# Moving the low weight parts by 64 bytes, spreading out a series, and splitting a last block in an fp32r encoder kernel

## The chip, the cores and the metric

The kernel runs on one core of a Trainium2 chip, as one program and one launch. The metric is the time on the device in microseconds (us), from start to end of one execution. The core has a matrix engine (PE, with its weight loads shown as PEld), a vector engine (DVE), an activation engine (ACT), GpSimd (POOL) and a queue engine (SP) that here only issues DMAs. Matmul results go to PSUM, which the kernel uses as eight banks of 512 fp32 columns on 128 partitions; all else lies in SBUF.

## The reference

The input is one sequence of 256 tokens of width 2048. Two layers follow each other, each with a residual addition, and a last norm ends it:

```python
h = rmsnorm(x, norm_w[0]);  x = x + mamba2_mixer(h, ...)
h = rmsnorm(x, norm_w[1]);  x = x + forgetting_attention_mixer(h, ...)
return rmsnorm(x, final_norm_w)        # x * rsqrt(mean(x*x) + 1e-6) * w
```

The Mamba-2 mixer projects to z, x, B, C (width 10240) and 64 step sizes dt, runs a causal convolution of four taps with SiLU, takes `dt = softplus(dt_raw + bias)`, runs the chunked state-space sum over 8 groups of 8 heads, gates with SiLU(z), applies a norm in each group, and projects 4096 back to 2048. The forgetting attention projects to q, k, v, z (4 x 4096) and 32 forget logits, takes `log_sigmoid` of these and their running sum, runs causal softmax attention with that sum as bias, gates with SiLU(z), and projects back. Everything is fp32.

## The kernel before, in words

**fp32 by parts.** Nearly all the weight products are made in the fp32r type, with each weight tile split into a high part `wh` (ACT, `act_hi`, L100) and a low part `wl` (DVE, `dve_lo`, L106: raw minus high). The activations are split the same way. A product is then the sum of high*high, low*high and high*low.

**The stream of weights.** Weights come in halves of 128 x 1024 fp32 (512 KB). `prep` (L130) takes a `raw` buffer (seven of them), issues the load on SP, and lets ACT and DVE make `wh` (five buffers) and `wl` (four buffers, `bufs=4` at L135 and L156). All three lie in the pool "weights". `raw`, `wh` and `wl` are each 4096 bytes a partition, so all of them start at the same place within 4096 bytes.

**The order of work.** The whole program is a list of parts (`run`, L162). A part is one half of a weight unit. For each part `run` first emits the preparation of the half that lies three ahead, then the part's matmuls, then its `post`, and then whatever was put off until now with `later(n, fn)` (L121), n counted in parts. The order that is emitted is a priority: a scheduler then sets the fixed order of each engine's queue from it, by when it reckons things to be ready. On the chip each queue runs in that order.

**Three kinds of parts.** `unit_t` (L190) makes a transposed output tile: the weight tile is the stationary operand, eight matmuls with `wh` on 512 columns (both activation parts side by side, L203) and eight with `wl` on 256 columns (L207). `units_a` (L267) has the activations stationary and the weights moving: twelve matmuls of 512 columns for a half, the `wl` ones last (L282), into one PSUM bank for each of the two token tiles. `sum_units` (L691) makes most of the two output projections (groups 0 to 5) by a Strassen-like scheme, from weight tiles that accumulating DMAs on POOL's queue add up in SBUF, six matmuls a part: for each p the three products high*wh, low*wh, high*wl (L711).

**Step sizes and forget gates.** `per_token` (L326) turns the 64 (or 32) columns to tokens and hands them to `decays` (L422) or `forget` (L800). Both call `log1p_exp` (L309): on DVE ten small dependent instructions after an Exp on ACT, L314 to L323, ending in the series of L320 to L323. Then come `dts` (L425) and `dta` (L430), and five parts later `decay_sums` (L435): small matmuls on `dta` (L440 on), a copy, and a write of the running sums to DRAM (`acs_d`).

**The sums by head.** `load_acs` (L519) reads the running sums of two heads back, broadcast to 128 partitions, into one of two `acsB` buffers, on POOL's DMA queue. `decay` (L561) makes exponentials from it on ACT (L566, L568), DVE multiplies (L572), and `y_pe` (L577) uses the product on PE (L585).

**The end.** The last output block (group 7, columns 1536 to 2047, `n == 3`) is made for the first token tile and then for the second (`by_token`). `finish` (L976) is called for each block and token tile after the sum into `xs` (L677). For the first three blocks it squares on ACT and multiplies by the norm weight on DVE. For the last it squares (L756), sums the four squares (L984), takes the power -0.5 (L114 on DVE, L115 on POOL), scales four quarters (two on DVE at L987 and L988, two on ACT at L990) and issues four output DMAs on SP (L992).

Of the kernel before, what the change touches and what calls it, by code (L numbers as in the profile page):

```python
# [63 lines left out]
def hybrid_kernel(ctx: ExitStack, tc: tile.TileContext, a):  # L64
# [7 lines left out]
    wp = pool("weights", 5)  # L72
    cp = pool("const", 1)
# [14 lines left out]
    nhalf = cp.tile([P, 2], F32, name="nhalf")  # L88
# [41 lines left out]
    def prep(u, h, pieces=1):  # L130


        raw = wp.tile([P, 1024], F32, tag="raw", name="raw", bufs=RAW)
        wh = wp.tile([P, 1024], F32R, tag="wh", name="wh")
        wl = wp.tile([P, 1024], F32R, tag="wl", name="wl", bufs=4)  # L135
        for i in range(pieces):
            c = slice(i * 1024 // pieces, (i + 1) * 1024 // pieces)
            nc.sync.dma_start(raw[:, c], u["src"][:, h * 1024 + c.start:h * 1024 + c.stop])
            act_hi(wh[:, c], raw[:, c])
            dve_lo(wl[:, c], raw[:, c], wh[:, c])  # L140
            if i + 1 < pieces:
                yield
        u["w"][h] = (wh, wl)

    def prep_sum(u):
# [10 lines left out]
        wl = wp.tile([P, 1024], F32R, tag="wl", name="wl", bufs=4)  # L156
# [110 lines left out]
    def units_a(srcs, act, post, by_token=False):  # L267


        held = {}  # L270
# [3 lines left out]
        def mm(n, tiles):  # L274
            if n == 0 and tiles[0] == 0:
                held["ps"] = [bank(psm, f"psa{t}") for t in range(T2)]
            wh, wl = us[n // 2]["w"][n % 2]
            for i, w in enumerate((wh, wh, wl)):
                for k2 in range(2):
                    c = slice(k2 * 512, k2 * 512 + 512)  # L280
                    for t in tiles:
                        nc.tensor.matmul(held["ps"][t], act(2 * n + k2, t)[i % 2], w[:, c],  # L282
                                         start=n == k2 == i == 0,
                                         stop=n == n_h - 1 and k2 == 1 and i == 2)

        parts = []
        for tiles in ((0,), (1,)) if by_token else ((0, 1),):
            for n in range(n_h):
                parts.append({"u": us[n // 2], "h": [n % 2],
                              "mm": lambda n=n, tiles=tiles: mm(n, tiles)})  # L290
            parts[-1]["post"] = lambda tiles=tiles: post(held["ps"], tiles)
# [17 lines left out]
    def log1p_exp(v, n, name):  # L309
# [10 lines left out]
        nc.vector.tensor_scalar(q, s2, 2.0 / 17, None, op0=ALU.mult)  # L320
        for d in (15, 13, 11, 9, 7, 5, 3):
            nc.vector.scalar_tensor_tensor(q, q, 2.0 / d, s2, op0=ALU.add, op1=ALU.mult)
        nc.vector.scalar_tensor_tensor(q, q, 2.0, s, op0=ALU.add, op1=ALU.mult)  # L323
        return q
# [40 lines left out]
    rst1 = cp.tile([P, 2], F32, name="rst1")  # L365
# [56 lines left out]
    def decays(v):  # L422
        v = v.rearrange("p t h -> p (t h)")
        l = log1p_exp(v, T2 * MH, "sp")
        nc.vector.scalar_tensor_tensor(dts.rearrange("p t h -> p (t h)"), v, 0.0, l,  # L425
                                       op0=ALU.max, op1=ALU.add)
# [3 lines left out]
        nc.vector.scalar_tensor_tensor(  # L430
            dta, dts, -1.0, na.unsqueeze(1).to_broadcast([P, T2, MH]),
            op0=ALU.mult, op1=ALU.mult)
        later(5, lambda: decay_sums(dta))
# [47 lines left out]
    def group_units(g):  # L481
# [37 lines left out]
        def load_acs(i):  # L519
            acs = lp.tile([P, 2, S], F32, tag="acsB", name="acsB", bufs=2)  # L520
# [149 lines left out]
    def out_units(w, act, groups, done, enter=None):  # L670

        parts = []
        for n in range(4):
            def post(pss, tiles, n=n):
                for t in tiles:
                    c = xs[:, t, n * 512:(n + 1) * 512]
                    nc.vector.tensor_tensor(c, pss[t], c, op=ALU.add)  # L677
                    if done is not None:
                        done(n, t)
# [11 lines left out]
    def sum_units(w, held, groups):  # L691
# [3 lines left out]
        for cp2 in range(2):  # L695
# [7 lines left out]
            def mm(u, form, name, start, stop, ps=ps):  # L703
# [96 lines left out]
    def forget(v):  # L800
        vf = small.tile([P, T2 * FH], F32, tag="vf", name="vf", bufs=1)
        nc.vector.tensor_copy(vf.rearrange("p (t h) -> p t h", t=T2), v)
        l = log1p_exp(vf, T2 * FH, "ls")
        lf = small.tile([P, T2, FH], F32, tag="lf", name="lf", bufs=1)
        nc.vector.scalar_tensor_tensor(lf.rearrange("p t h -> p (t h)"), vf, 0.0, l,
                                       op0=ALU.min, op1=ALU.subtract)
        later(5, lambda: forget_sums(lf))
# [168 lines left out]
    def finish(n, t):  # L976
        square(n, t)
        c = xs[:, t, n * 512:(n + 1) * 512]
        fw = lay2["fw"]
        if n < 3:  # L980
            nc.vector.tensor_tensor(c, c, fw, op=ALU.mult)
            return
        r = small.tile([P, 1], F32, tag="fr", name="fr")
        nc.vector.tensor_reduce(r, lay2["sq"][:, t, :], axis=mybir.AxisListType.X, op=ALU.add)  # L984
        rsqrt(r, r, 1.0 / D, EPS)
        quarter = [xs[:, t, m * 512:(m + 1) * 512] for m in range(4)]
        nc.vector.tensor_scalar(quarter[2], quarter[2], r, None, op0=ALU.mult)  # L987
        nc.vector.scalar_tensor_tensor(c, c, r, fw, op0=ALU.mult, op1=ALU.mult)  # L988
        for m in range(2):
            nc.scalar.activation(quarter[m], quarter[m], AF.Copy, scale=r)  # L990
        for m in (2, 0, 3, 1):
            nc.sync.dma_start(a["out"][t * P:(t + 1) * P, m * 512:(m + 1) * 512], quarter[m])  # L992
# [100 lines left out]
```

## Time and profile before

| | |
|---|---|
| median of 3 runs | 1622.39 us (1622.38 to 1625.78) |
| the profiled execution | 1623.64 us, of which its span is 1621.8 us |
| busy, share of the span | PE 99%, PEld 85%, DVE 78%, ACT 62%, POOL 8% |
| granted TensorE clock | 0.998 |
| DMA | 347.70 MB, 214 GB/s on average |
| matmuls and weight loads | 8514 each |

The span is what the profile covers; the rest of an execution's time lies around it. A row of the timeline gives the start, the time to the end of the last of its merged instructions, the engine, the line and operation, the tile written and those read, the shapes, the count, and in brackets how long the engine had been idle and what ended that. Matmuls are pipelined: one that takes 0.39 us from start to end starts 0.23 us after the one before it. The pace of the engine is therefore read from starts, and not from durations.

### The profile page before, as it was taken

To read this page: it belongs to the slowest core of one execution; us is meant where nothing else is said; L and a number is where in the kernel's file an instruction comes from. 1 tells how busy PE (TensorE), PEld (TensorE's weight loads), DVE (VectorE), ACT (ScalarE), POOL (GpSimd) and SP (SyncE) were. 2 spreads that over 40 slices of the span, in tenths; PEclk is the share of its full clock that TensorE was granted. 3 is DMA by queue.
4 is the path that set the end of the run, shared out by engine and by line. 5 is a ranking of instruction groups with operands and counts; after the bars stand their busy time and mean duration, and the time that the engine had idled before them with its cause. 6 is when DMAs were issued, how large, how long until landed. Compare 5 with 4: busy or idle time off the path is not lost.

```text
span 1621.8 us, 23800 instructions
## 1 busy us (share of the span) xinstructions
PE 1598.9 (99%) x8514; PEld 1371.1 (85%) x8514; DVE 1263.8 (78%) x2091; ACT 1002.7 (62%) x1609; POOL 122.1 (8%) x166
## 2 busy tenths in 40 slices
PE   8999999999999999999999999999999999999997
PEld 6788888888888888888888888888888888888886
DVE  6898989898989897757767677676787676786776
ACT  7677777676767665645555566565565565665653
POOL 0000111011101110000000010100000000101000
PEclk9999999999999999999999999999999999999999
DMA  9666789778977897555555687865887866878752
GB/s 354 203 204 195 200 251 227 256 192 250 234 250 192 246 229 229 173 183 196 179 189 179 204 227 228 223 225 177 223 233 214 238 205 188 223 220 238 222 180 98
DMA packets 96937, 347.70 MB, mean 214 GB/s; under 512 B 11153, under 2 KB 11793, under 8 KB 96817
## 3 DMA queue, kind: packets, MB, share of 16 engines
q1 hardware_dynamic: 78768, 282.09, 51.3%
q0 software_dynamic: 18048, 64.07, 21.6%
q8 instruction: 67, 1.10, 0.3%
q14 instruction: 54, 0.43, 0.1%
HBM read 343.92 MB, written 2.20 MB: 213 GB/s over the span
## 4 chain that ended last, share of the span: by engine, by line
PE 88%; issue 4%; DMA 3%; DVE 2%; ACT 1%; POOL 0%; SPq 0%; ACTq 0%; POOLq 0%; DVEq 0%
PE pst L203 30%; PE psa L282 23%; PE pst L207 16%; PE psx L711 7%; PE psz L711 4%; PE psv L711 2%; PE py L585 2%; DVE wl L106 1%; DMA raw<-in_wf_q 1%; PE ppt L922 1%; DMA cst<-in_consts 1%; DMA xs<-in_x 1%; PE pyt L640 0%; PE pof L590 0%; PE pxa L538 0%
## 5 line engine op out<-in xcount | busy, mean ns | idle before, releaser
L106 DVE TENSOR_TENSOR wl<-raw,wh 128x1024 fp32r<-128x1024 f32 (+1 forms) x453 | 552.1, 1219 | 212.2 <-PE pst L207 85.8
L100 ACT ACTIVATE wh<-raw 128x1024 fp32r<-128x1024 f32 (+1 forms) x453 | 478.1, 1057 | 352.3 <-PE pst L203 133.3
L203 PE MATMUL pst<-x,wh 128*128 128x512 f32 x2272 | 575.3, 394 | 3.0 <-ACT v L102 3.0
L203 PEld LDWEIGHTS pst<-x,wh 128*128 128x128 f32 x2272 | 412.0, 188 | 80.1 <-ACT v L102 3.6
L207 PEld LDWEIGHTS pst<-x,wl 128*128 128x128 f32 x2272 | 309.8, 190 | 22.4
L207 PE MATMUL pst<-x,wl 128*128 128x256 f32 x2272 | 316.6, 282 | 0.0
L282 PE MATMUL psa<-wh,x 128*128 128x512 f32 x1024 | 260.2, 395 | 0.0
L282 PEld LDWEIGHTS psa<-wh,x 128*128 128x128 f32 x1024 | 189.7, 188 | 40.6 <-issue 1.9
L106 DVE TENSOR_TENSOR wl<-sum_a,wh 128x1024 fp32r<-128x1024 f32 x96 | 117.2, 1221 | 36.9 <-PE pst L207 23.7
L100 ACT ACTIVATE wh<-sum_a 128x1024 fp32r<-128x1024 f32 x96 | 101.6, 1058 | 64.0 <-PE psa L282 27.1
L282 PE MATMUL psa<-wl,x 128*128 128x512 f32 x512 | 137.1, 390 | 1.2 <-DVE wl L106 1.2
L282 PEld LDWEIGHTS psa<-wl,x 128*128 128x128 f32 x512 | 96.0, 188 | 21.6 <-DVE wl L106 1.7
L106 DVE TENSOR_TENSOR wl<-sum_b,wh 128x1024 fp32r<-128x1024 f32 x48 | 58.6, 1222 | 21.9 <-PE pst L207 11.6
L100 ACT ACTIVATE wh<-sum_b 128x1024 fp32r<-128x1024 f32 x48 | 50.9, 1061 | 31.7 <-PE psa L282 9.6
L153 POOL DMA_DIRECT2D sum_a<-in_wf_s x36 | 31.2, 866 | 338.7 <-DVE wl L106 238.5
L263 ACT COPY rest<-pst 128x256 f32<-128x256 f32 (+2 forms) x146 | 52.2, 358 | 3.1 <-PE pst L252 1.5
L566 ACT ACTIVATE ee<-acsB,beta 128x128 f32<-128x128 f32 x128 | 42.6, 391 | 10.6 <-DMA acsB<-acs_d 6.2
L153 POOL DMA_DIRECT2D sum_a<-in_wm_s x36 | 31.4, 873 | 203.1 <-DVE xT L468 70.3
L468 DVE SCALAR_TENSOR_TENSOR xT<-cu,vec,xT 128x255 f32<-128x255 f32 (+2 forms) x96 | 45.5, 474 | 0.4 <-ACT xT L463 0.4
L908 ACT ACTIVATE uu<-uu,mx 128x128 f32<-128x128 f32 x64 | 28.5, 446 | 25.7 <-DVE mx L906 25.7
L711 PE MATMUL psx<-wh,ghf 128*128 128x512 f32 x96 | 38.3, 399 | 0.0
L711 PE MATMUL psx<-wh,glf 128*128 128x512 f32 x96 | 37.8, 393 | 0.0
(312 smaller groups left out, 2025.8 us busy)
## 6 DMA issues: line engine op xcount, KB each, us to landing
raw<-in_wm_t SPq DMA_DIRECT2D x90, 512.0 KB, 5.0
raw<-in_wm_z SPq DMA_DIRECT2D x64, 512.0 KB, 5.3
raw<-in_wf_q SPq DMA_DIRECT2D x64, 512.0 KB, 4.5
raw<-in_wf_k SPq DMA_DIRECT2D x64, 512.0 KB, 4.6
raw<-in_wf_v SPq DMA_DIRECT2D x64, 512.0 KB, 4.1
raw<-in_wf_z SPq DMA_DIRECT2D x64, 512.0 KB, 4.4
sum_a<-in_wm_s POOLq DMA_DIRECT2D x36, 512.0 KB, 5.9
sum_a<-in_wf_s POOLq DMA_DIRECT2D x36, 512.0 KB, 5.6
```

Of the source, the lines that this page charges most:

```text
L100: nc.scalar.activation(out, in_, AF.Copy)
L106: nc.vector.tensor_tensor(out, in_, hi.bitcast(F32), op=ALU.subtract)
L153: nc.gpsimd.dma_start(u["sums"][name], src, accum_op=ALU.add)
L203: nc.tensor.matmul(ps, wh[:, k8 * P:k8 * P + P], v[:, k].rearrange("p i s -> p (i s)"), start=k == 0, stop=False)
L207: nc.tensor.matmul(ps[:, S:], wl[:, k8 * P:k8 * P + P], v[:, k, 0], start=False, stop=k == KT - 1)
L263: nc.scalar.copy(rest, ps[:n, S:])
L282: nc.tensor.matmul(held["ps"][t], act(2 * n + k2, t)[i % 2], w[:, c], start=n == k2 == i == 0, stop=n == n_h - 1 and k2 == 1 and i == 2)
L468: nc.vector.scalar_tensor_tensor(acc[:, j:], u[:, :S - j], cw(3 - j), acc[:, j:], op0=ALU.mult, op1=ALU.add)
L566: nc.scalar.activation(ee[:, j, t, :], st["acs"][i][:, j, t * P:t * P + P], AF.Relu, scale=-1.0, bias=beta[:, t, h:h + 1])
L585: nc.tensor.matmul(st["py"][t][:, c], m[:, j, t, :], st["xd"][:, t, c], start=True, stop=True)
L711: nc.tensor.matmul(ps[name], y[:, form, :], w[:, c], start=start and p == i == 0, stop=stop and p == 1 and i == 2, skip_group_check=True)
L908: nc.scalar.activation(uu[:, c:c + n], uu[:, c:c + n], AF.Exp, bias=mx[:, t:t + 1], accum_out=sm[:, t:t + 1])
```

## The change

**Low parts.** `wl` moves from the pool "weights" to a pool of its own, "lows", with four buffers as before. A pool "between" lies ahead of it and holds two small tiles, `nhalf` and `rst1`, that the pool "const" held: 32 bytes a partition each, so every `wl` starts 64 bytes further on than it did, and `raw` and `wh` stay where they were. What lies behind "const" starts where it did, but for the pools behind "small", which grows by two 32-byte buffers.

**Series.** `log1p_exp` stops after the square s2; the series, and what uses it, is emitted one part later, and `decay_sums` and `forget_sums` four parts after that.

**First group's running sums.** For group 0 `load_acs` takes its tile from the `gh` buffers of the pool "forms", which hold nothing yet, in place of the two `acsB` buffers.

**Order in `sum_units`.** The six matmuls of a part go by product and then by p, so that both `wl` products come last.

**The end.** The last block goes in three pieces: first token tile (512 columns), second token tile columns 0 to 255, then 256 to 511, the two halves in the same PSUM bank. The sum of the first three squares is formed after the third block. The last square (or its two halves) is added to it. Of the first tile only quarter 0 is scaled at once; quarter 3 is emitted after the addition of the last half, quarters 2 and 1 after the second tile's power.

```diff
+    mp = pool("between", 1)
+    lo = pool("lows", 4)
     cp = pool("const", 1)
...
-    nhalf = cp.tile([P, 2], F32, name="nhalf")
+    nhalf = mp.tile([P, 2], F32, name="nhalf")
...
-        wl = wp.tile([P, 1024], F32R, tag="wl", name="wl", bufs=4)
+        wl = lo.tile([P, 1024], F32R, tag="wl", name="wl")
...
         def mm(n, tiles, a, b):
+            if n == a == 0:
+                for t in tiles:
+                    held[t] = bank(psm, f"psa{t}")
...
-                        nc.tensor.matmul(held["ps"][t], act(2 * n + k2, t)[i % 2], w[:, c],
+                        nc.tensor.matmul(held[t][:, a:b], act(2 * n + k2, t)[i % 2], w[:, c],
...
-        for tiles in ((0,), (1,)) if by_token else ((0, 1),):
+        for tiles, a, b in ((((0,), 0, 512), ((1,), 0, 256), ((1,), 256, 512)) if by_token else
+                            (((0, 1), 0, 512),)):
...
-        nc.vector.tensor_scalar(q, s2, 2.0 / 17, None, op0=ALU.mult)
...
+        def series():
+            nc.vector.tensor_scalar(q, s2, 2.0 / 17, None, op0=ALU.mult)
+            for d in (15, 13, 11, 9, 7, 5, 3):
+                nc.vector.scalar_tensor_tensor(q, q, 2.0 / d, s2, op0=ALU.add, op1=ALU.mult)
+            nc.vector.scalar_tensor_tensor(q, q, 2.0, s, op0=ALU.add, op1=ALU.mult)
+            done(q)
+        later(1, series)
...
-        later(5, lambda: decay_sums(dta))
+            later(4, lambda: decay_sums(dta))
...
-            acs = lp.tile([P, 2, S], F32, tag="acsB", name="acsB", bufs=2)
+            if g == 0:
+                acs = gp.tile([P, 896], F32, tag="gh", name="acsB0")
+                acs = acs[:, :2 * S].rearrange("p (h s) -> p h s", h=2)
+            else:
+                acs = lp.tile([P, 2, S], F32, tag="acsB", name="acsB", bufs=2)
...
-                for p in range(2):
-                    gh, gl = held[u["g"]][p]
-                    c = slice(p * 512, p * 512 + 512)
-                    for i, (y, w) in enumerate(((gh, wh), (gl, wh), (gh, wl))):
+                for i, w in enumerate((wh, wh, wl)):
+                    for p in range(2):
+                        y = held[u["g"]][p][i % 2]
+                        c = slice(p * 512, p * 512 + 512)
...
+            if n == 2:
+                lay2[f"sum{t}"] = r = small.tile([P, 1], F32, tag="fr", name="fr")
+                nc.vector.tensor_reduce(r, lay2["sq"][:, t, :3], axis=mybir.AxisListType.X,
+                                        op=ALU.add)
+                nc.vector.tensor_scalar(r, r, D * EPS, None, op0=ALU.add)
...
+        if b0 == 512 and t == 1:
+            lay2["scale"](3)
+        q = small.tile([P, 1], F32, tag="fq", name="fq")
+        junk = sp.tile([P, 512], F32, tag="zth", name="junkf")
+        nc.scalar.activation(junk[:, :b0 - a0], xs[:, t, 1536 + a0:1536 + b0], AF.Square,
+                             accum_out=q)
+        if b0 < 512:
+            nc.vector.tensor_tensor(r, r, q, op=ALU.add)
+            return
+        nc.vector.tensor_scalar(q, q, r, 1.0 / D, op0=ALU.add, op1=ALU.mult)
+        nc.gpsimd.tensor_tensor(r, q, nhalf[:, :1], op=ALU.pow)
+        if t == 0:
+            lay2["scale"] = scale
+            scale(0)
+        else:
+            for m in (2, 1):
+                lay2["scale"](m)
+            for m in (2, 0, 3, 1):
+                scale(m)
```

`scale(m)` scales quarter m on ACT (0 and 1) or DVE (2 and 3) and issues its output DMA.

More of the change, by code (lines that the diff above doesn't have):

```diff
@@ L272, in units_a, with mm @@
         us = [{"src": src, "w": [None, None]} for src in srcs]
-        def mm(n, tiles):
-            if n == 0 and tiles[0] == 0:
-                held["ps"] = [bank(psm, f"psa{t}") for t in range(T2)]
+        def mm(n, tiles, a, b):
+            if n == a == 0:
+                for t in tiles:
+                    held[t] = bank(psm, f"psa{t}")
             wh, wl = us[n // 2]["w"][n % 2]
@@ L673, in out_units, with post @@
         for n in range(4):
-            def post(pss, tiles, n=n):
+            def post(pss, tiles, a=0, b=512, n=n):
                 for t in tiles:
-                    c = xs[:, t, n * 512:(n + 1) * 512]
-                    nc.vector.tensor_tensor(c, pss[t], c, op=ALU.add)
-                    if done is not None:
+                    c = xs[:, t, n * 512 + a:n * 512 + b]
+                    nc.vector.tensor_tensor(c, pss[t][:, a:b], c, op=ALU.add)
+                    if enter is not None:
+                        done(n, t, a, b)
+                    elif done is not None:
                         done(n, t)
@@ L974, in load_fw, with finish, scale @@
         nc.gpsimd.dma_start(fw, a["fnw"][n * 512:(n + 1) * 512].partition_broadcast(P))
-    def finish(n, t):
-        square(n, t)
-        c = xs[:, t, n * 512:(n + 1) * 512]
+    def finish(n, t, a0, b0):
         fw = lay2["fw"]
+        part = lambda m: xs[:, t, m * 512:(m + 1) * 512]
         if n < 3:
-            nc.vector.tensor_tensor(c, c, fw, op=ALU.mult)
-            return
[L983 to L992, printed above, removed]
+            square(n, t)
+            nc.vector.tensor_tensor(part(n), part(n), fw, op=ALU.mult)
+            if n == 2:
[3 more added lines that the diff above has]
+                nc.vector.tensor_scalar(r, r, D * EPS, None, op0=ALU.add)
+            return
+        r = lay2[f"sum{t}"]
+        def scale(m):
+            if m < 2:
+                nc.scalar.activation(part(m), part(m), AF.Copy, scale=r)
+            elif m == 2:
+                nc.vector.tensor_scalar(part(2), part(2), r, None, op0=ALU.mult)
+            else:
+                nc.vector.scalar_tensor_tensor(part(3), part(3), r, fw, op0=ALU.mult,
+                                               op1=ALU.mult)
+            nc.sync.dma_start(a["out"][t * P:(t + 1) * P, m * 512:(m + 1) * 512], part(m))
+        if b0 == 512 and t == 1:
[12 more added lines that the diff above has]
+            scale(0)
+        else:
+            for m in (2, 1):
+                lay2["scale"](m)
+            for m in (2, 0, 3, 1):
+                scale(m)
```

39 lines of the change are left out of this document (19 added, 20 removed).

## The prediction

> **What bounds the kernel now.** I read the page first (busy shares and the chain that ended last), then what PE waited for, then the timeline around each of its waits, and last the end.
>
> ```profile
> span 1621.8 us, 23800 instructions
> PE 1598.9 (99%) x8514; PEld 1371.1 (85%) x8514; DVE 1263.8 (78%) x2091; ACT 1002.7 (62%) x1609; POOL 122.1 (8%) x166
> ...
> PE 88%; issue 4%; DMA 3%; DVE 2%; ACT 1%; POOL 0%; SPq 0%; ACTq 0%; POOLq 0%; DVEq 0%
> ...
> L207 PE MATMUL pst<-x,wl 128*128 128x256 f32 x2272 | 316.6, 282 | 0.0
> ```
>
> PE is busy for 1598.9 of 1621.8 us, and the chain is PE's. So time can come from two places only: the 23 us in which PE stands (10 of them behind its last matmul, below), or the pace at which it runs. Two of the waits that the profile lists for PE (total, times, longest):
>
> ```profile
> PE py L585 <- DVE ee L572: 1.5, 1, 1.5
> PE psa L282 <- DVE wl L106: 1.2, 1, 1.2
> ```
>
> Each is a single wait, both in the first group, as the timeline shows further down. Now the pace, from starts:
>
> ```profile
> 1302.96 1.98 PE L203 MATMUL pst<-x,wh 128*128 128x512 f32 x8
> 1304.78 1.11 PE L207 MATMUL pst<-x,wl 128*128 128x256 f32 x8
> 1305.73 2.00 PE L203 MATMUL pst<-x,wh 128*128 128x512 f32 x8
> ```
>
> Eight matmuls of 512 columns take 1.82 us (228 ns each), eight of 256 columns 0.95 us (119 ns). Half of 228 is 114, so a short matmul with `wl` as its stationary operand costs 5 ns more than its columns alone would, 2272 times: 11.4 us. Something that goes with each weight load is in that, and the shift touches these loads.
>
> **The change part by part.** *Low parts 64 bytes on.* No instruction is added or taken away; the address of 2272 stationary tiles changes (L207), and that of the moving operand where `wl` is that. Does an address that is no multiple of 128 bytes cost PE anything? The nearest rows are attention's small products: adding up the tiles of the pools puts that pool 32 bytes past a multiple of 128, and both operands of L884 and L885 lie in it.
>
> ```profile
> 751.97 0.28 PE L884 MATMUL psc<-kh,qh 128*128 128x256 f32 x1
> 752.08 0.28 PE L885 MATMUL psc<-kl,qh 128*128 128x256 f32 x1
> 752.20 1.98 PE L203 MATMUL pst<-x,wh 128*128 128x512 f32 x8
> ```
>
> They run 0.11 and 0.12 us apart, 115 ns on average: no dearer than the 119 ns of L207, and a little under it. But there both operands have the same offset, and behind the change `wl` and `x` differ by 64 bytes, which no row shows. So the bounds are 5 ns less for each of the 2272 (-11.4 us, the long matmul's pace) and as much more (+11.4 us, nothing shows more). I take 0, as the rows with an odd start are nearest and differ by a few ns in a count of two. DVE's writing of `wl` and the loads of `raw` keep their work; they run beside PE.
>
> *The series one part later.* In the first layer `wl` came late to the first half of z:
>
> ```profile
> 51.35 0.28 DVE L322 SCALAR_TENSOR_TENSOR sp_q<-sp_q,sp_s 128x128 f32<-128x128 f32 x1
> 51.55 0.48 DVE L468 SCALAR_TENSOR_TENSOR xT<-cu,vec,xT 128x254 f32<-128x254 f32 x1
> 51.95 0.28 DVE L323 SCALAR_TENSOR_TENSOR sp_q<-sp_q,sp_s 128x128 f32<-128x128 f32 x1
> 52.15 0.48 DVE L468 SCALAR_TENSOR_TENSOR xT<-cu,vec,xT 128x253 f32<-128x253 f32 x1
> 52.54 0.28 DVE L425 SCALAR_TENSOR_TENSOR dts<-v,sp_q 128x128 f32<-128x128 f32 x1
> 52.74 1.22 DVE L106 TENSOR_TENSOR wl<-raw,wh 128x1024 fp32r<-128x1024 f32 x1
> 53.88 0.28 DVE L430 SCALAR_TENSOR_TENSOR dta<-dts,na 128x128 f32<-128x128 f32 x1
> 54.08 0.42 DVE L264 TENSOR_TENSOR cu<-pst,rest 128x256 f32<-128x256 f32 x1
> ```
>
> ```profile
> 55.14 0.65 PE L440 MATMUL pc<-cst,dta 128*64 128x128 f32 x4
> ```
>
> DVE runs these back to back, and each step of the series holds it 0.20 us (51.35 to 51.55). Were the three that stand here (51.35, 51.95, 52.54) behind the L106 at 52.74 in place of ahead of it, `wl` would come 0.6 us earlier, and of PE's 1.2 us wait 0.6 would be left. But something else is late next: `dta` was done at 54.16 and PE used it at 55.14, 1 us later. With PE 0.6 us ahead and three to five steps of 0.2 us now behind, that slack is used up, and L440 could wait for some 0.6 us; what is queued behind it on PE is the next half of z. So between -1.2 (wait gone, L440 in time) and +0.3 us (L440 waits longer than L282 did). I take -0.6, as the slack of 1 us covers about the rest. In the second layer the same step has no wait among PE's, so it brings 0 there.
>
> *Group 0's own buffers.* POOL issued the third load when ACT let go of the first buffer, and ACT then stood:
>
> ```profile
> 68.29 0.40 ACT L566 ACTIVATE ee<-acsB,beta 128x128 f32<-128x128 f32 x1 [1.11 <-DMA acsB<-acs_d]
> ...
> 73.09 0.40 ACT L566 ACTIVATE ee<-acsB,beta 128x128 f32<-128x128 f32 x1 [1.75 <-DMA acsB<-acs_d]
> ```
>
> ```profile
> 71.08 0.43 DVE L473 SCALAR_TENSOR_TENSOR xT<-cu,xT 128x256 f32<-128x256 f32 x1 [4.63 <-ACT cu L470]
> ...
> 77.42 0.68 DVE L572 TENSOR_TENSOR ee<-ee,cb 128x512 f32<-128x512 f32 x1
> ```
>
> ```profile
> 78.24 0.96 PE L585 MATMUL py<-xd,ee 128*128 128x64 f32 x7 [1.46 <-DVE ee L572]
> ```
>
> The 1.75 us go, since loads three and four no longer wait. The 1.11 us are for the second load, which had its buffer, and stay. PE's 1.46 us follow from DVE, which worked without a stop from 71.08, when a tanh released it, to the L572 that PE wants. That stretch begins before the wait that goes. So the gain reaches PE only if the scheduler, seeing the exponentials ready earlier, puts L572 further ahead: between 0 and -1.46 us, and I take -0.5, nearer to 0 by the timeline. Behind PE's wait stands the next unit's L203. The `gh` buffers are wanted long after.
>
> *Order in `sum_units`.* The low part is needed after four matmuls and not after two, 0.46 us later. No wait for it stands among PE's at L711, so 0.
>
> *The end.* Before:
>
> ```profile
> 1611.26 0.61 PE L282 MATMUL psa<-wl,ghf 128*128 128x512 f32 x2
> ...
> 1612.27 0.75 DVE L988 SCALAR_TENSOR_TENSOR xs<-xs,fr,fw 128x512 f32<-128x512 f32 x1
> ...
> 1612.93 0.68 DVE L677 TENSOR_TENSOR xs<-psa,xs 128x512 f32<-128x512 f32 x1
> 1613.71 0.63 ACT L756 ACTIVATE junkb<-xs 128x512 f32<-128x512 f32 x1 [0.51 <-DVE xs L677]
> ...
> 1614.65 0.15 DVE L114 TENSOR_SCALAR fr<-fr 128x1 f32<-128x1 f32 x1
> 1614.89 0.55 POOL L115 TENSOR_TENSOR fr<-fr,nhalf 128x1 f32<-128x1 f32 x1 [3.06 <-DVE fr L114]
> 1615.48 1.34 ACT L990 ACTIVATE xs<-xs,fr 128x512 f32<-128x512 f32 x2 [1.05 <-POOL fr L115]
> ```
>
> From the last matmul's end (1611.87) to the scaling (1615.48) are 3.61 us, of which DVE spent 1.06 on the first tile's quarters before it could add. After: an addition of 256 columns (0.42, as L264 above) with a hand-off of 0.1 on each side (1613.61 to 1613.71), a square of 256 columns with the reading of its sum (between half of 0.63 and all of it; 0.52 as an estimate), one DVE step of 0.15, POOL with its hand-offs 0.68 (1614.80 to 1615.48): 1.97 us, so 1.64 less. Against it: 24 matmuls of 119 ns in place of 12 of 228 ns are 0.12 us. And the second half goes into the bank that DVE is reading the first half from. No row of before shows an engine reading a bank while PE writes it, so the price lies between 0 and a full wait: last matmul 0.28, addition 0.42 and two hand-offs (0.10 and 0.14, the latter from L572's end at 78.10 to 78.24), less one normal step of 0.12, or 0.8 us. I take the 0.8, since the two halves are one tile to whatever orders the accesses: -1.64 + 0.12 + 0.8 = -0.7. The four outputs of the second tile are issued as before. Ends: -1.5 without that wait, and 0 where the first tile's quarter 3 (0.75, L988) still stands ahead of the last addition.
>
> That reading and writing one bank at once is no choice of order alone is said by the Trainium skill ("PSUM — Partial Sum Buffer", PSUM bank collisions raise a hardware error): two engines on one bank and quarter of the partitions collide, whatever columns they touch, so software has to keep them apart. By that rule the halves run one behind the other and the end gives 0.7; without it, 1.5. No run here shows it yet.
>
> The sum: 0 - 0.6 - 0.5 + 0 - 0.7 = -1.8 us. The profiled execution took 1623.64 us (span 1621.8 and 1.84 around it), so 1621.8 for it; it lies 1.25 us above the median of 1622.39, which gives 1620.6. About 0.2% (3.2 us, below 1619.15 or above 1625.6) is what a measurement of this kernel can tell from no change, so this is no change by that measure.
>
> **The rivals.** *The loads of `wl` run faster.* If the 5 ns of each short matmul come from the weight load and the moving operand reading the same place in step, 64 bytes part them: -11.4 us, together 1609.2. For it: the surplus goes with the loads and not with the columns, so it is PE's own. Against: L885's 115 ns with operands in step. The Trainium skill ("SBUF — State Buffer", Who interferes with whom) says that only the port pair of VectorE and GpSimd causes contention and that PE waits on nobody; by it this rival is worth 0, and the 5 ns are not explained. *The small edits give all they could:* -1.2, -1.46 and -1.5, or 1618.2. For it: each was a single wait with a nameable cause. *Slower: the shifted loads run dearer.* If a weight load from an address off a multiple of 128 costs what the short matmul already has over it once more, 5 ns on 2272, the sum is 1620.6 + 11.4 = 1632.0; from 2.2 ns each on it outweighs the 1.8 us and the 3.2 us of the measure together. Against: L884 and L885 again. *The change does nothing in the first group:* L440 takes over L282's wait and L572 stays: -0.7 alone, 1621.7.
>
> **How the numbers follow.** The forecast (1620.6; own range 1618.2 to 1622.7, from -4.2 to +0.3): 0.42. Faster loads: 0.28. All small edits in full: 0.12. Nothing in the first group: 0.08. Dearer loads: 0.10. Over 0.2% faster are the second and the third and a tenth of the forecast (0.04): 0.44; slower: 0.10; within: 0.46. The range leaves out the dearer loads and the faster loads that give over 11.4 us with the small edits: 1608.5 to 1623.
>
> **What would show it.** Right: L207 still 119 ns from start to start; L282's wait for `wl` below 0.5 us with at most as much at L440; ACT without the 1.75 us at its third `acsB`; PE standing about 0.8 us between the two halves of the last block; the scaling 0.7 us nearer to the last matmul of before. Wrong: short matmuls at 114 ns or at 124, in all stretches of the trace alike; or a new wait of over 1 us on PE in the first 100 us.

## The result, and the profile after

The changed kernel takes 1629.32 us (median of 6 runs, 1627.29 to 1630.98), the kernel before 1623.23 us (6 runs, 1622.38 to 1625.78). The ratio is 1.0038, with a 95% interval of 1.0026 to 1.0050: 6 us slower, where 1.8 us faster was forecast. The profiled execution of after took 1629.76 us. The head of its page, and the two of PE's waits in it that matter (total, times, longest):

```profile
span 1628.0 us, 23828 instructions
...
PE 1607.2 (99%) x8526; PEld 1371.2 (84%) x8526; DVE 1264.0 (78%) x2095; ACT 1002.0 (62%) x1611; POOL 121.8 (7%) x166
```

```profile
PE py L600 <- DVE ee L587: 2.4, 1, 2.4
...
PE psa L286 <- DVE xs L692: 0.5, 1, 0.5
```

The span is 6.2 us longer, and PE's busy time 8.3 us with 12 matmuls more. (A busy time counts modelled ends, so it names the place and not the exact size.) To find where the 6.2 us arise, the span is cut at two conversions of weight halves on ACT that both kernels have, the 41st and the 601st of 621. Their rows in the timeline of before, and then of after:

```profile
121.62 1.05 ACT L100 ACTIVATE wh<-raw 128x1024 fp32r<-128x1024 f32 x1
...
1539.46 1.06 ACT L100 ACTIVATE wh<-raw 128x1024 fp32r<-128x1024 f32 x1 [0.77 <-PE psx L711]
```

```profile
123.23 1.05 ACT L102 ACTIVATE wh<-raw 128x1024 fp32r<-128x1024 f32 x1
...
1545.08 1.06 ACT L102 ACTIVATE wh<-raw 128x1024 fp32r<-128x1024 f32 x1 [0.55 <-PE psx L728]
```

The beginning, to the 41st, is 1.6 us longer (123.23 for 121.62). The long middle takes 1421.9 us in place of 1417.8, 4.0 more. The rest is 82.9 in place of 82.3 us. So most of the loss is made in the middle. There PE even waits less than before. The largest group of its waits in the middle, before and then after (total, times, longest):

```profile
PE pst L203 <- ACT v L102: 3.0, 3, 1.3
```

```profile
PE pst L205 <- ACT v L104: 0.9, 2, 0.4
```

With all idle times of PE over 0.15 us in the middle taken off, 1419.9 us are left in place of 1414.1. So the pace of PE cost 5.8 us there, and shorter waits hid nearly 2 us of it. Four rows of the timeline in the same place of the first output projection, before and then after:

```profile
630.46 1.98 PE L282 MATMUL psa<-wh,x 128*128 128x512 f32 x8
632.28 1.07 PE L282 MATMUL psa<-wl,x 128*128 128x512 f32 x4
633.18 1.98 PE L282 MATMUL psa<-wh,x 128*128 128x512 f32 x8
635.00 1.07 PE L282 MATMUL psa<-wl,x 128*128 128x512 f32 x4
```

```profile
635.07 1.99 PE L286 MATMUL psa<-wh,x 128*128 128x512 f32 x8
636.90 1.10 PE L286 MATMUL psa<-wl,x 128*128 128x512 f32 x4
637.83 2.00 PE L286 MATMUL psa<-wh,x 128*128 128x512 f32 x8
639.67 1.10 PE L286 MATMUL psa<-wl,x 128*128 128x512 f32 x4
```

The four matmuls through which `wl` moves take 0.93 us from start to start (636.90 to 637.83) in place of 0.90, and the eight with `wh` behind them 1.84 in place of 1.82. The group of the first kind has grown by 4.2 us in busy time, while that of the short matmuls, in which `wl` is stationary (316.6 us before), has shrunk. First the row of before, then the two of after:

```profile
L282 PE MATMUL psa<-wl,x 128*128 128x512 f32 x512 | 137.1, 390 | 1.2 <-DVE wl L106 1.2
```

```profile
L286 PE MATMUL psa<-wl,x 128*128 128x512 f32 x512 | 141.3, 397 | 0.0
...
L209 PE MATMUL pst<-x,wl 128*128 128x256 f32 x2272 | 313.5, 281 | 0.0
```

The rows of the transposed parts that answer to those at 1302.96 us of before:

```profile
1304.86 1.98 PE L205 MATMUL pst<-x,wh 128*128 128x512 f32 x8
1306.68 1.11 PE L209 MATMUL pst<-x,wl 128*128 128x256 f32 x8
1307.62 0.63 PE L728 MATMUL psx<-wh,ghf 128*128 128x512 f32 x2
```

Eight long ones take 1.82 us as before, eight short ones 0.94 in place of 0.95.

**The first group.** PE's wait for `wl` at 52 us is gone (idle 0.0 in the L286 row above). What became of it shows further on, in the timeline of after, one fence each for DVE, PE and ACT, and then what follows:

```profile
56.87 0.30 DVE L440 SCALAR_TENSOR_TENSOR dta<-dts,na 128x128 f32<-128x128 f32 x1
...
71.25 0.43 DVE L484 SCALAR_TENSOR_TENSOR xT<-cu,xT 128x256 f32<-128x256 f32 x1 [4.40 <-ACT cu L481]
...
77.57 0.69 DVE L587 TENSOR_TENSOR ee<-ee,cb 128x512 f32<-128x512 f32 x1
```

```profile
57.65 0.65 PE L451 MATMUL pc<-cst,dta 128*64 128x128 f32 x4
...
78.41 1.08 PE L600 MATMUL py<-xd,ee 128*128 128x64 f32 x8 [2.43 <-DVE ee L587]
79.32 0.60 PE L553 MATMUL pxa<-cst,xT 128*128 128x128 f32 x2
79.57 3.57 PE L205 MATMUL pst<-x,wh 128*128 128x512 f32 x8
```

```profile
68.33 1.28 ACT L581 ACTIVATE ee<-acsB,beta 128x128 f32<-128x128 f32 x4 [3.71 <-DMA acsB<-acs_d]
```

`dta` is ready at 57.2 us, 3 us later than before. From it come the running sums, their write to DRAM and their load, on which ACT stands 3.71 us (68.33). A tanh that DVE wants (L481) is queued behind that on ACT, so DVE stands 4.40 us, and then works without a stop to the L587 for which PE waits. That wait was 1.46 us and is 2.43 in this execution. And behind it eight long matmuls take 3.40 us (79.57 to the next row's start at 82.97), where eight of before took 1.91. The windows of after show the granted TensorE clock there, in the third column from the end, at half:

```profile
78.00:80.00 2.00, 1.59 (x11) 1.62 (x12) 2.00 (x4) 1.86 (x5) 0.00 (x0) 0.84 0.76 295
80.00:82.00 2.00, 2.00 (x6) 1.52 (x6) 2.00 (x3) 1.43 (x4) 0.00 (x0) 0.50 0.87 315
```

**The end.** From the timeline of after, PE and then DVE:

```profile
1615.58 0.40 PE L286 MATMUL psa<-wh,ghf 128*128 128x256 f32 x2
...
1617.68 0.51 PE L286 MATMUL psa<-wh,ghf 128*128 128x256 f32 x2 [0.52 <-DVE xs L692]
...
1618.96 0.40 PE L286 MATMUL psa<-wl,ghf 128*128 128x256 f32 x2
```

```profile
1619.57 0.42 DVE L692 TENSOR_TENSOR xs<-psa,xs 128x256 f32<-128x256 f32 x1
...
1621.51 0.49 DVE L1014 TENSOR_SCALAR xs<-xs,fr 128x512 f32<-128x512 f32 x1 [0.67 <-POOL fr L1030]
```

PE stands 0.52 us between the halves, until the addition has read the first. From the start of the second tile's last matmuls to its scaling are 5.93 us (1615.58 to 1621.51). Before they were 6.49: twelve matmuls that began at 1608.99, and the scaling at 1615.48.

So two theories stood for test. A: the 64 bytes set PE's pace. B: the loss is made in the first group, by the later series and the half clock behind PE's wait.

### The profile page after: what moved, and what is told of

It is laid out like the page before. It is cut to its first block, busy times and chain, and to the rows that moved or that the text cites. A ratio compares the mean times of both kernels' runs of the same rounds, so it can differ in the third digit from the quotient of the medians.

```text
span 1628.0 us, 23828 instructions
## 1 busy us (share of the span) xinstructions
PE 1607.2 (99%) x8526; PEld 1371.2 (84%) x8526; DVE 1264.0 (78%) x2095; ACT 1002.0 (62%) x1611; POOL 121.8 (7%) x166
## 4 chain that ended last, share of the span: by engine, by line
PE 87%; issue 7%; DVE 3%; DMA 2%; ACT 1%; POOL 1%; SPq 0%; POOLq 0%; ACTq 0%; DVEq 0%
PE pst L205 29%; PE psa L286 25%; PE pst L209 15%; PE psx L728 7%; PE psz L728 4%; PE psv L728 2%; PE py L600 2%; DVE wl L108 1%; PE ppt L941 1%; DMA cst<-in_consts 1%; DMA xs<-in_x 1%; PE pxa L553 0%; PE po L959 0%; PE psc L900 0%; DMA xt<-in_xT 0%
## 5 line engine op out<-in xcount | busy, mean ns | idle before, releaser
L286 PE MATMUL psa<-wh,x 128*128 128x512 f32 x1024 | 261.6, 397 | 0.0
L286 PEld LDWEIGHTS psa<-wh,x 128*128 128x128 f32 x1024 | 189.9, 188 | 43.0 <-issue 3.3
L286 PE MATMUL psa<-wl,x 128*128 128x512 f32 x512 | 141.3, 397 | 0.0
L286 PEld LDWEIGHTS psa<-wl,x 128*128 128x128 f32 x512 | 95.8, 188 | 22.2 <-DVE wl L108 0.2
L108 DVE TENSOR_TENSOR wl<-sum_b,wh 128x1024 fp32r<-128x1024 f32 x48 | 58.7, 1223 | 22.2 <-PE pst L209 11.4
L600 PEld LDWEIGHTS py<-xd,ee 128*128 128x128 f32 x256 | 33.2, 192 | 5.2 <-ACT wh L102 2.8
L108 DVE TENSOR_TENSOR wl<-sum_c,wh 128x1024 fp32r<-128x1024 f32 x24 | 29.4, 1224 | 10.6 <-issue 4.7
```

The costliest lines, as they stand in the source:

```text
L108: nc.vector.tensor_tensor(out, in_, hi.bitcast(F32), op=ALU.subtract)
L286: nc.tensor.matmul(held[t][:, a:b], act(2 * n + k2, t)[i % 2], w[:, c], start=n == k2 == i == 0, stop=n == n_h - 1 and k2 == 1 and i == 2)
L600: nc.tensor.matmul(st["py"][t][:, c], m[:, j, t, :], st["xd"][:, t, c], start=True, stop=True)
```

## The experiments

Two numbers are read beside each ratio: the middle of the span (41st to 601st conversion, 1417.8 us before; where two kernels are close, also what is left of it without PE's idle times of over 0.15 us, 1414.1 us before), and the mean time from start to start, taken over all such matmuls of the trace behind 121 us: short ones with stationary `wl` (119.0 ns before) and blocks' matmuls with moving `wl` (227.0 ns before).

**The 64 bytes alone** (low_64_alone):

```diff
+    mp = pool("between", 1)
+    lo = pool("lows", 4)
-        wl = wp.tile([P, 1024], F32R, tag="wl", name="wl", bufs=4)
+        wl = lo.tile([P, 1024], F32R, tag="wl", name="wl")
```

(and `nhalf`, `rst1` in "between", as in the change)

> The kernel before with only the two new pools: every wl starts 64 bytes further on, nothing else of the change. Theory A (the start of wl against the other operands of PE sets PE's pace): in the profile after, a moving wl costs 234 ns from start to start in place of 227 (some 640 matmuls outside of the summed units, +4.5 us), the long matmuls behind it a little more, and a short matmul with stationary wl 118 in place of 119 ns (-3 us); with the summed units 4 to 5 us in all, so about 1627.5 us against 1623.2, spread evenly over the whole span, and no new wait in the first group. Theory B (the loss is made in the first group, by the later series and the halved clock behind PE's longer wait at 78 us): 1623.2 us, and 227 ns for a moving wl.

Measured: 1629.15 us, ratio 1.0036 (1.0024 to 1.0048). The middle took 1423.5 us, 5.6 more; moving `wl` 233.3 ns, short matmuls 117.5. Theory A holds; this one edit is as dear as the whole change, by the intervals. Could another engine that reads or writes the shifted buffers be what holds PE up? The trace of this run speaks against it. The 24 matmuls with moving `wl` beside which DVE, ACT and POOL work for less than a tenth of the time take 235.9 ns (226.7 before). The 518 beside which DVE writes no `wl` take 233.3.

**All but the 64 bytes** (after_low_back): `wl`, `nhalf` and `rst1` back in their old pools, the rest as changed.

> The changed kernel with wl, nhalf and rst1 back where they were; the later series, group 0's own buffers, the order in the summed units and the new end stay. Theory A: 4 to 5 us less than the changed kernel, about 1624.8 us: what is left over the kernel before is the first group (PE's wait of 2.4 us at 78 us and the half clock behind it, some +1.1 us) less the end (-0.4). Theory B: as the changed kernel, 1629.3 us.

Measured: 1622.82 us, ratio 0.9998 (0.9989 to 1.0008). The middle took 1417.4 us, with 227.0 and 119.0 ns. The four other edits together make no difference that can be measured, and theory B falls: without the 64 bytes the loss is gone.

**Everything 64 bytes on** (all_64):

```diff
+    mp = pool("between", 1)
     bp = pool("big", 1)
+    gap = mp.tile([P, 16], F32, name="gap")
```

> The kernel before with 64 unused bytes ahead of everything that it allocates: all operands of PE start 64 bytes further on, and no two of them move against each other. Theory A (only the offset of one operand against the others counts): the time and the pace of before, 1623.2 us, 227 ns for long and 119 ns for short matmuls. Theory C (a start off a multiple of 128 bytes is dearer by itself): a moving wl at 234 ns as in the profile after, +4.5 us, and the moving wh and x too, up to 7 ns on each of some 4000 long matmuls: 1628 to 1651 us.

Measured: 1623.38 us, ratio 0.9996 (0.9987 to 1.0004); 227.0 and 119.0 ns, middle 1416.8 us. The group of the moving `wl` is back to the size of before:

```profile
L285 PE MATMUL psa<-wl,x 128*128 128x512 f32 x512 | 137.2, 390 | 1.2 <-DVE wl L109 1.2
```

A start 64 bytes off a multiple of 128 costs nothing by itself (theory C falls). What counts is where one operand starts against another.

**128 bytes** (low_128), **32** (low_32), **256** (low_256) and **512** (low_512), each by what lies in "between":

```diff
+    gap = mp.tile([P, 32], F32, name="gap")
```

```diff
-    nhalf = cp.tile([P, 2], F32, name="nhalf")
+    nhalf = mp.tile([P, 2], F32, name="nhalf")
```

```diff
-    cum_q = cp.tile([P, T2, FH], F32, name="cum_q")
+    cum_q = mp.tile([P, T2, FH], F32, name="cum_q")
```

and for 512 bytes `nhalf`, `rst1`, `cum_q` and an unused tile of 192 bytes.

> The kernel before with 128 unused bytes ahead of wl: the same two new pools, but the start of wl stays a multiple of 128 bytes. Theories A and C, in the form that what counts is the place within 128 bytes: 1623.2 us, 227 and 119 ns. Rival D (what counts is that raw, wh and wl start at the same place within 4096 bytes, or that wl has a pool of its own): dearer as with 64 bytes, about 1627.5 us.

> The kernel before with wl 32 bytes further on (only nhalf lies ahead of it). So far 64 bytes cost 5.3 us and 128 bytes 11.2 us, while moving all operands together by 64 cost nothing: what counts is where wl starts against the other operands. Theory E (all operands of PE started at multiples of 512 bytes of each other, the size of one stationary tile in a partition, and the best pace needs that): dearer, by 2 to 11 us, with moving wl above 227 ns. Theory F (only the bits from 64 bytes upward count): as before, 1623.9 us, moving wl at 227 ns.

> The kernel before with wl 256 bytes further on (cum_q lies ahead of it). Theory E (a whole stationary tile of 512 bytes is the period): dearer, 5 us or more, as 128 bytes were. Theory G (the period is 256 bytes): as before, 1623.9 us, 227 ns for a moving wl and 119 for a short matmul.

> The kernel before with wl 512 bytes further on (nhalf, rst1, cum_q and 192 unused bytes lie ahead of it). Theory E, and G too: as before, 1623.9 us, 227 and 119 ns. Rival D (a start at the same place within 4096 bytes as raw and wh is what counts, or that wl has a pool of its own): dearer, by 5 us or more.

Measured:

| `wl` further on by | ratio (95%) | middle, us | short, stationary `wl`, ns | blocks, moving `wl`, ns |
|---|---|---|---|---|
| 0 (before) | 1 | 1417.8 | 119.0 | 227.0 |
| 32 bytes | 1.0074 (1.0060 to 1.0087) | 1429.0 | 118.3 | 233.9 |
| 64 bytes | 1.0036 (1.0024 to 1.0048) | 1423.5 | 117.5 | 233.3 |
| 128 bytes | 1.0072 (1.0060 to 1.0085) | 1428.8 | 120.3 | 231.1 |
| 256 bytes | 1.0002 (0.9992 to 1.0011) | 1417.0 | 119.0 | 227.0 |
| 512 bytes | 1.0016 (1.0007 to 1.0025) | 1421.1 | 119.0 | 227.2 |

The expectation for 128 bytes (as before) was wrong; that miss led to the other sizes. 256 bytes give the pace of before in every kind of matmul: the pace repeats after 256 bytes (theory G). Theory E, a period of 512, falls, and D, that a pool of its own costs, falls with it. With 128 and 512 bytes the pools behind "const" moved too (by 128 and 192); no operand of the matmuls counted here lies there. The 512 bytes have nearly the pace of before, but 1.0016 in time. The profile shows one event:

```profile
1039.39 1.06 ACT L104 ACTIVATE wh<-raw 128x1024 fp32r<-128x1024 f32 x1 [4.34 <-DMA raw<-in_wf_q]
...
1042.60 3.57 PE L207 MATMUL pst<-x,wh 128*128 128x512 f32 x8 [2.08 <-ACT v L106]
```

A load came late, PE stood 2.08 us, and the eight matmuls behind ran at half clock (3.37 us to the next row's start at 1045.97, in place of 1.82). That explains only half of the 3.3 us by which its middle is longer. For PE's waits there are no longer in all than before. The group of waits that the 2.08 us belong to, in this kernel and then before:

```profile
PE pst L207 <- ACT v L106: 2.9, 2, 2.1
```

```profile
PE pst L203 <- ACT v L102: 3.0, 3, 1.3
```

So the half clock is 1.5 us of it. The rest, some 1.9 us, is pace: the long matmuls cost 0.5 ns more in all stretches of the trace (229.4 in place of 228.9 ns in the transposed parts, 227.8 in place of 227.3 for moving `wh`). What brings these 0.5 ns was not tried.

**The 64 bytes where `wl` is stationary, and only there** (by_use_64), and the same with 192 (by_use_192):

```diff
+    def low(at):
+        t = wp.tile([P, 1088], F32R, tag="wl", name="wl", bufs=4)
+        return t[:, at // 4:at // 4 + 1024]
-        wl = wp.tile([P, 1024], F32R, tag="wl", name="wl", bufs=4)
+        wl = low(u.get("low", 0))
-        e, b, s, s2, q = tl("e"), tl("b"), tl("s"), tl("s2"), tl("q")
+        e, b, s, s2, q = tl("e"), tl("b"), tl("s"), tl("e"), tl("b")
```

(the units of the transposed parts carry "low": 64, or 192, the others nothing)

> The kernel before with wl buffers 256 bytes longer: a half whose wl will be stationary (transposed parts) starts 64 bytes into its buffer, one whose wl will be moving starts at 0. To make room, two of the scratch tiles of the step sizes' series share their buffers with dead ones. Theory G (wl's start modulo 256 against the other operands, use by use, sets PE's pace): the short matmuls at 117 to 118 ns and a transposed part at 2769 in place of 2781 ns, as with wl shifted everywhere, 284 times 11.3 ns or 3.2 us less; moving wl at 227 ns as before; 1619.6 us. Rival H (a shift costs where the pattern changes from part to part, so mixing is worse than either): 1623 to 1628 us.

> As the kernel with 64 bytes by use, but 192 bytes (64 short of the next 256). If only the distance within 256 bytes counts, whichever operand is ahead: the same short matmuls of 117 to 118 ns and 1619.6 us. If it counts which operand is ahead: another pace for the transposed parts, anywhere between the 119 ns of before less 6 (the long matmul's pace) and the 121 ns seen at 128 bytes, 1616 to 1630 us. Moving wl 227 ns in both cases.

Measured: 64 by use takes 1619.77 us, ratio 0.9976 (0.9968 to 0.9985), the middle 1414.0 us, 3.9 less (3.5 without PE's idle times); short matmuls 117.3 ns, moving `wl` 227.1. It beats both kernels. The short matmuls gain 1.7 ns each, 2272 times: 3.9 us, which is the whole gain (2056 of them lie in the middle: 3.5 us). Rival H falls. 192 by use: 1623.04 us, ratio 1.0000 (0.9991 to 1.0009): the short ones gain as well (117.9 ns), but the long matmuls of the same parts cost 229.7 ns in place of 228.9. So 64 ahead and 64 behind are not the same.

**The series alone** (series_alone) and **group 0's buffers alone** (buffers_alone), each with only that part of the change's diff:

> The kernel before with only the series one part later. As the changed kernel's profile has it: PE's wait of 1.2 us for wl at 52 us is gone, dta comes 3 us later against the work around it, so the running sums and the exponentials come later too, and PE's wait for the first product of them (0 to 2.4 us in the profiles so far) takes back 1 us or more: no gain by the median, 1622 to 1624 us. The forecast's step: 0.6 us less, no new wait.

> The kernel before with only group 0's running sums in the buffers of gh. All six loads are issued back to back, ACT's wait of 1.75 us before the third is gone; the first load is no earlier, so the first product that PE waits for is no earlier than the first four exponentials allow. The forecast's step: 0.5 us less (between 0 and 1.46), with PE's wait at 78 us shorter than the 0 to 2.4 us seen with the old buffers: 1622.3 us by it. Rival: that wait hangs on the first load and on DVE's line of work, and stays: 1622.8.

Measured: the series 1624.33 us, ratio 1.0003 (0.9994 to 1.0012), the buffers 1624.99 us, 1.0007 (0.9998 to 1.0016). Neither shows a gain, though the 0.6 us forecast for the series lie within its interval. In the first PE's wait for `wl` is gone and its wait for the first product is 2.56 us. In the second all six loads go at once, and the third exponential waits for none. The first still does, and the whole line behind it with it (timeline of buffers_alone: POOL, ACT, DVE, PE):

```profile
61.06 3.26 POOL L525 DMA_DIRECT2D acsB<-acs_d  x6 [3.66 <-DMA acs_d<-acs]
```

```profile
67.13 1.28 ACT L570 ACTIVATE ee<-acsB,beta 128x128 f32<-128x128 f32 x4 [4.42 <-DMA acsB<-acs_d]
```

```profile
71.94 0.43 DVE L473 SCALAR_TENSOR_TENSOR xT<-cu,xT 128x256 f32<-128x256 f32 x1 [5.33 <-ACT cu L470]
```

```profile
79.10 1.68 PE L589 MATMUL py<-xd,ee 128*128 128x64 f32 x8 [2.16 <-DVE ee L576]
```

How much the beginning varies by itself is seen in the thirteen kernels here in which neither of these two edits is made, and whose work there differs at most in addresses: the 41st conversion comes between 120.18 and 124.47 us, 121.85 on average, and PE's wait for the first product (L585 before) reaches from none in the list to 2.4 us. With both edits it came at 120.67 and 123.23 us, with the series alone at 123.02, with the buffers alone at 124.10. Effects of half a microsecond in this stretch can't be told from that.

**The end alone** (end_alone), and with its halves in two PSUM banks (end_two_banks):

```diff
-            if n == a == 0:
+            if n == 0:
                 for t in tiles:
                     held[t] = bank(psm, f"psa{t}")
```

> The kernel before with only the new end: last block of the second token tile in two halves in one bank, first three squares summed early, the first tile's scaling spread. From the trace of the changed kernel: from the start of the second tile's last matmuls to its scaling 5.93 us in place of 6.49, the outputs behind it 0.17 us longer: 0.4 us less, 1623.5 against 1623.9 us, PE standing 0.5 us between the halves. The forecast of 0.7 us less would be 1623.2; the bound of 1.5 us 1622.4. If the outputs that now wait in line behind the first tile's quarters take back the gain: 1623.9 or more.

> The new end alone, with the two halves of the last block in different PSUM banks. With one bank PE stood 0.5 us before the second half until the addition of the first had read it. If the shared bank is the cause: no such wait, the scaling 0.5 us nearer to the start of the second tile's last matmuls than with one bank (5.4 in place of 5.9 us; 6.5 before), and by the end of the trace 0.9 us less than before. If the wait comes from the order in which things are issued: PE stands as long in this kernel. In the whole time either is at the edge of what shows: 1621.9 to 1623.4 us.

Measured: ratios 1.0000 (0.9990 to 1.0010) and 1.0000 (0.9989 to 1.0011). The stretch from the 601st conversion to the end tells more: 82.04 us in both. In the eight profiles with the old end and with moving `wl` at the pace of before it is 82.26 to 82.44, so the new end brings 0.3 us. (In all but the 64 bytes it is 82.24, 0.1 less than before.) But the middle of the kernels with the new end is longer: without PE's idle times 1414.5 to 1414.6 us in these two and in all but the 64 bytes, against 1414.0 to 1414.1 in the five kernels with the old end and the pace of before in every kind of matmul. That takes the 0.3 us back. These kernels have two 32-byte buffers more in "small", which moves what lies behind it; whether this is the cause was not tried. With two banks PE has no wait between the halves, and nothing is won by it. PE and then DVE in the timeline of end_two_banks:

```profile
1608.81 0.40 PE L284 MATMUL psa<-wh,ghf 128*128 128x256 f32 x2
...
1611.44 0.40 PE L284 MATMUL psa<-wl,ghf 128*128 128x256 f32 x2
```

```profile
1611.72 0.75 DVE L1003 SCALAR_TENSOR_TENSOR xs<-xs,fr,fw 128x512 f32<-128x512 f32 x1 [0.69 <-POOL fr L1017]
1612.39 0.15 DVE L1014 TENSOR_TENSOR fr<-fr,fq 128x1 f32<-128x1 f32 x1
1612.46 0.48 DVE L1001 TENSOR_SCALAR xs<-xs,fr 128x512 f32<-128x512 f32 x1
1612.85 0.42 DVE L681 TENSOR_TENSOR xs<-psa,xs 128x256 f32<-128x256 f32 x1
...
1614.79 0.48 DVE L1001 TENSOR_SCALAR xs<-xs,fr 128x512 f32<-128x512 f32 x1 [0.67 <-POOL fr L1017]
```

The last matmul ends at 1611.84, and DVE adds at 1612.85. In between it scales two quarters of the first tile (0.75 and 0.48 us) that stand ahead of the addition in its queue. From the first matmul of the half to the scaling are 5.98 us, as with one bank, where 5.4 were expected. So the shared bank did make PE wait, as the expectation said, and the wait cost nothing, since DVE was late next.

**The 64 bytes with the order in the summed units** (low_64_order): the kernel of the first run, and the loops of L711 as changed.

> All wl 64 bytes on, as in the first of these runs, and the order in the summed units with both wl products last. From 121 us to the end the kernel with 64 bytes alone ran 6.0 us longer than before, the changed kernel 4.5, and the changed kernel without the 64 bytes as before. If the order halves the number of switches between operands at different offsets and so saves 1.4 us of the shift's cost: 4.5 us there, about 1.0028 by the ratio in place of 1.0036. If the 1.4 us come from another of the edits: 6.0 and 1.0036.

Measured: 1628.56 us, ratio 1.0026 (1.0016 to 1.0035), the middle 1421.5 us, 2.0 less than the 64 bytes alone (the two intervals overlap, so this rests on the middle, which lies between 1416.5 and 1417.9 us in the eight kernels that keep the pace of before and have no late load). But a good half of the 2.0 us lies in one group of PE's waits, which ranges from 0.9 to 3.0 us over the kernels here. With the 64 bytes alone and then with the order:

```profile
PE pst L205 <- ACT v L104: 2.2, 3, 1.3
```

```profile
PE pst L205 <- ACT v L104: 1.1, 3, 0.6
```

Without PE's idle times the middle is 1420.0 us with the 64 bytes alone and 1419.1 with the order, against 1414.1 before. So in pace the order gives back some 1 us of 6 in this profile, less than the expected 1.4. Without the shift no gain is seen (1414.6 against 1414.1, with the other edits in it).

**Both gains together** (by_use_and_end): 64 by use, and the end in two banks.

> The 64 bytes by use (3.9 us less by itself) together with the new end in two banks, without the later series, group 0's buffers and the order in the summed units. If the two add up: 4.3 to 4.8 us less than the kernel before, ratio 0.9970 to 0.9974. If the end's gain is lost in what follows it: 0.9976 as with the 64 bytes by use alone.

Measured: 1620.89 us, ratio 0.9981 (0.9971 to 0.9990). The middle took 1414.7 us and the rest 82.04, so both parts are in it, but without PE's idle times the middle is 1412.0 us against 1410.6 with 64 by use alone, so that again more is lost there than the end brings; the beginning came out at 123.21 us, with eight long matmuls at half clock behind PE's wait for the first product. By the times it can't be told from the 64 bytes by use alone.

## Why the prediction was wrong

**The 64 bytes, taken at 0: the step that failed.** The sum went by L884 and L885 as the "nearest rows": two small products whose operands both lie off a multiple of 128, in the same pool. The prediction said itself that "both operands have the same offset" there, and that no row showed two that differ. Moving all operands together is just what costs nothing (all_64), so those rows could price nothing of this edit. Second, the bounds of 11.4 us on either side covered the 2272 stationary uses alone; "that of the moving operand where `wl` is that" was named and never given a price. The loss is there. From the mean starts of the 64 bytes alone times the counts of each kind:

| kind of part | matmuls | before, us | 64 bytes on, us |
|---|---|---|---|
| transposed (`wl` stationary) | 2272 + 2272 | 790.3 | 787.8 |
| blocks (`wh`, `wl` moving) | 1280 + 640 | 436.3 | 443.4 |
| summed units (`wh`, `wl` moving) | 672 + 336 | 231.7 | 234.0 |

That is -2.5, +7.1 and +2.3 us, 6.9 in all, against 6.5 that the middle without PE's idle times and the rest of that profile lost (6.0 and 0.5). In the blocks not only moving `wl` became dearer (227.0 to 233.3 ns), but moving `wh` beside it too (227.3 to 229.7).

**The rivals on the shift.** "The loads of `wl` run faster" had the right place and sign and was 1.5 ns in size, not 5; alone it is the 3.9 us of by_use_64. "The shifted loads run dearer" had the right sign, twice the size (11.4 us for 5.8) and the wrong matmuls: its 124 ns never came, nor at any shift tried. Of the Trainium skill the prediction had quoted that PE waits on nobody ("SBUF — State Buffer", Who interferes with whom), where it is also said that PE's two reading ports, for the moving operand and for the weight load, are independent. A wait on another engine is not what these runs show, as the dear matmuls are as dear with no other engine at work (235.9 ns). But the place of `wl` against PE's other operands was changed and the pace of moving `wl` went from 227.0 to 233.9 ns (32 bytes), which two independent reads would not lead one to expect; the measurement decides. Which two accesses get in each other's way was not tried apart (`x` or the forms moved alone), so the mechanism behind the pace stays open.

**The series, -0.6.** L282's wait went, all of it, and L451 did not wait in its place. But the prediction looked for what is late next at the first use of `dta` and stopped there. Late next was the road of the running sums through DRAM, 11 us further on. In the profiles of after and of the series alone PE's lead was spent waiting for the first product (2.43 and 2.56 us); in that of all but the 64 bytes, with the same later series, that wait was 1.15 us. So how much of the lead is lost there is not shown. By the ratio the edit is worth +0.5 us, from -1.0 to +1.9.

**Group 0's buffers, -0.5.** The 1.75 us went as said. The timeline argument beside the term, that DVE's stretch "begins before the wait that goes", was the right one and asked for 0. And the 1.46 us of PE that the term was a share of is one execution's number: in others it was anything from none listed to 2.4. By the ratio the edit is worth +1.1 us, from -0.3 to +2.6.

**The order, 0.** Right by itself.

**The end, -0.7.** In its own stretch it is -0.1 to -0.3, and the longer middle of the kernels with it takes that back. The wait between the halves was there (0.52 for 0.8 us), but it isn't what decides: the prediction's own other end, "0 where the first tile's quarter 3 (0.75, L988) still stands ahead of the last addition", came nearly true, with quarter 2 behind it. The rule on PSUM banks of the Trainium skill ("PSUM — Partial Sum Buffer", PSUM bank collisions raise a hardware error) was brought in to choose between 0.7 and 1.5. In the runs PE waited with one bank (0.52 us) and not with two, which fits it, and the gain is the same.

So the four small terms, -1.8 in the sum, are -0.3 us together (0.9998; -1.8 to +1.3 by the interval), and the shift, 0 in the sum, is +5.8 alone (1.0036), of which the new order of the summed units gives back some 1 us.

**What the sum had no term for.** Behind PE's wait at 78 us its clock was at half, and the eight matmuls there took 1.5 us more than before. In the profile of after that is most of the 1.6 us of the beginning. But all_64 and by_use_and_end have it too, without one edit of the first group, and in the latter the wait is 1.44 us, no longer than the 1.46 of before. So it is no mark of the change.

## What to carry to other kernels

When a buffer is moved, price the place of each operand against the operand that PE reads beside it, use by use, stationary and moving: here 64 bytes were worth -1.7 ns in one use and +6.3 ns in the other, out of 119 and 227. A row prices an edit only if it varies what the edit varies; two operands moved together say nothing on one moved alone. Where a wait goes, follow the chain until it meets PE again, through DRAM too, before booking the gain, and look at several executions before taking a share of a single wait.

## What the runs showed of the hardware that was not expected

The pace of fp32r matmuls here depends on where their operands start against each other, modulo 256 bytes: 227.0 ns at 0 and 256 for 512 columns with moving `wl`, 231 to 234 at 32, 64 and 128; for 256 columns with stationary `wl` 119.0 at 0, 117.5 at 64 and 120.3 at 128.

The long matmuls beside them change with them: moving `wh` beside a `wl` shifted by 64 bytes went from 227.3 to 229.7 ns, most in the first of eight behind `wl` (226.7 to 231.6) and least in the last (227.0 to 227.4).

A wait of PE of 1.4 to 2.6 us can be followed by half the clock (the first 20 us of the kernel left out here). Behind waits of 1.44, 2.08, 2.16, 2.39, 2.43 and 2.56 us in six kernels (both gains together, 512 bytes, buffers, all 64, after, series) the long matmuls came 427 ns apart for up to 3.4 us, at a granted clock of 0.50. Behind one of 1.46 us (before), one of 2.18 (the series alone, at 1043 us) and one of 2.2 (the end alone) they did not. So the length of the wait alone does not decide it. The Trainium skill ("TensorE: Matmul & The Clock Gate", What's actually happening) has half the clock after an idle window of about 3.4 us that runs free of the work; here gaps shorter than that were enough.
